# A float32 gather, a token-major router and a 24th weight tile in a two-block model with 32 experts

## The chip, the cores and the metric

One core of one Trainium2 chip. The metric is the device time of one execution in microseconds; the figure for a kernel is the median of its runs.

## The reference

Two blocks on x of 256 tokens by 1024: a hybrid layer (four mixers, then a gated FFN), and a block of pooling with differential attention, cross attention and a mixture of experts. The change lies in the last part:

```python
logits = (xt @ w_router + b_router).astype(jnp.float32)   # 256 x 32
top_val, top_idx = lax.top_k(logits, TOP_K)               # TOP_K = 4
gates = jax.nn.softmax(top_val, axis=-1)
...
hb = clamped_swiglu(xb @ w_gu[e] + b_gu[e])    # xb: the tokens of expert e, w_gu[e]: 1024 x 2048
yb = hb @ w_down[e] + b_down[e]                # w_down[e]: 1024 x 1024
return yb * g[:, None].astype(yb.dtype)        # added into the tokens' rows
```

where xt is x, normalised by its root mean square and a gain. Everything is float32, so one expert has 12 MiB of weights and the 32 experts 384 MiB.

## The kernel before

All of the first block and the attention come first, to about 750 us; the rest of the run is the mixture of experts. x lies in x_t, two halves of 128 tokens by 1024.

**Router.** hT is x transposed and scaled. Eight products lps (L1301) give the logits with experts on the partitions, four partial sums side by side; ScalarE copies them (lsb, L1304), and two products lp with ident4 (L1307) add the partial sums and turn them to tokens on partitions. rm is 1/rms. VectorE makes the logits lg (L1312), the top 8 and their indices (L1358, L1361), casts the indices (L1364), compares them with iota_e into oh (L1369) and sums that to selb, the mask of chosen experts (L1372). pos (L1376 to L1378) counts, by a triangular matrix, each token's place among its expert's. seed (L1337) first adds x into the four accumulators acc.

**Gather.** Each expert has CAP = 64 places. For two experts at a time, one_hot (L1447) builds Sg, a bf16 matrix that holds a 1 where a token has a place; a chunk (L1472) is x's 128 columns times Sg. So that bf16 products are exact enough, x times 1/rms is split ahead into three bf16 parts xs: POOL multiplies and subtracts (L1346, L1348, L1350), ScalarE rounds (L1347, L1349). A chunk is six products, and ScalarE or VectorE evacuates it into xgg (L1478, L1476).

**Experts.** front(e) is gue (L1529), eight pieces of weights of 1 MiB, each with four float32 products of 512 columns; swiglu transposes (gte, L1545) and activates; dn_product (dne, L1571) takes four pieces of 1 MiB; scatter (L1581) adds the result into acc. The program writes gue of expert e+1 ahead of dne of expert e. The chunks of the next two experts stand between the pieces of dne of every even expert; those of experts 0 and 1 stand in gue of expert 0. A stop near 1530 us belongs to the overflow branch after expert 25, where SP reads the largest count.

**Weight tiles.** Each piece is loaded by SP's queue (ld in in_turn, L1493 and L1495) in the order of the program into a tile of slot_tile. The string SLOTS names the pool of each following tile, cyclically: 23 letters. A letter is a pool of one buffer, but "x" has two and "p" six. The pools x and p exist from the start of the kernel; the others lie where earlier stages' tiles lay. A load waits for the last reader of its buffer, and as SP issues in order, everything behind it waits too.

```python
SLOTS = "xxolkmnpppgfhppdeijpcba"
pool = slots[SLOTS[slot[0] % len(SLOTS)]]
return pool.tile([P, 2 * D], F32, tag="raw", name=f"raw{rawc[0]}")
```

b_down, 32 by 1024, is loaded after expert 1's weights by load_b_down into a corner of x_t (bd4), and add_b_down reads it after dne of expert 2 and after dne of expert 4. gs, u_ and gT, small results of an expert, lie in x_t as well, which nobody reads once it is split and seeded.

Of the kernel before, what the change touches and what calls it, by code (L numbers as in the profile page):

```python
# [22 lines left out]
P = 128  # L23
# [8 lines left out]
SLOTS = "xxolkmnpppgfhppdeijpcba"  # L32
# [11 lines left out]
def kernel(ctx: ExitStack, tc: tile.TileContext, A, out, probe=None, stop=None):  # L44
# [1266 lines left out]
    for b in range(2):  # L1311
        last["V"] = V.scalar_tensor_tensor(lg[:, b, :], lp2[:, b * NE:(b + 1) * NE], rm[:, b:b + 1], brt,  # L1312
                                           op0=ALU.mult, op1=ALU.add)
# [20 lines left out]
    def seed():  # L1334
        for b in range(2):
            for h in range(2):
                PE.matmul(acc[b][h], ident, x_t[:, b, half(h)], start=True, stop=False)  # L1337


    xsp = [mp.tile([P, 2, D], BF16, name=f"xs{i}") for i in range(3)]  # L1340
    xr = small.tile([P, D], F32, tag="xg", name="xr", bufs=1)
    for h in range(2):
        for b in range(2):
            hi, mid, lo = (t[:, b, half(h)] for t in xsp)
            rest = xr[:, half(b)]
            G.tensor_scalar(rest, x_t[:, b, half(h)], rm[:, b:b + 1], 0.0, op0=ALU.mult, op1=ALU.add)  # L1346
            S.copy(hi, rest)  # L1347
            G.tensor_tensor(rest, rest, hi, op=ALU.subtract)  # L1348
            S.copy(mid, rest)  # L1349
            G.tensor_tensor(lo, rest, mid, op=ALU.subtract)  # L1350
# [3 lines left out]
    i8 = small.tile([P, 2, 8], U32, tag="i8s", name="i8s", bufs=1)  # L1354
    fi = small.tile([P, 2, TOPK], F32, tag="fi", name="fi", bufs=1)
    st_ = small.tile([P, 2, 8], F32, tag="st_", name="st_", bufs=1)
    for b in range(2):
        V.max(out=t8[:, b, :], in_=lg[:, b, :])  # L1358
    V.tensor_scalar(st_[:, :, 4:5], t8[:, :, 0:1], -1.0, None, op0=ALU.mult)
    for b in range(2):  # L1360
        V.max_index(i8[:, b, :], t8[:, b, :], lg[:, b, :])  # L1361
        S.activation(st_[:, b, 0:TOPK], t8[:, b, 0:TOPK], AF.Exp, bias=st_[:, b, 4:5],
                     accum_out=st_[:, b, 5:6])
    V.tensor_copy(fi, i8[:, :, 0:TOPK])  # L1364
    oh = small.tile([P, 2, NE, TOPK], F32, tag="SG", name="oh", bufs=1)
# [9 lines left out]
    seed()  # L1375
# [6 lines left out]
    def gates():  # L1382
        V.reciprocal(st_[:, :, 6:7], st_[:, :, 5:6])
        for b in range(2):
            V.tensor_scalar(st_[:, b, 0:TOPK], st_[:, b, 0:TOPK], st_[:, b, 6:7], None, op0=ALU.mult)
            V.tensor_tensor(oh[:, b], oh[:, b], st_[:, b, 0:TOPK].unsqueeze(1).to_broadcast([P, NE, TOPK]),
                            op=ALU.mult)
        V.tensor_reduce(out=gate, in_=oh, axis=AX.X, op=ALU.add)

        V.tensor_scalar(gateh, gate, 0.5, None, op0=ALU.mult)  # L1390

        rest = oh[:, 0].rearrange("p e k -> p (e k)")[:, :2 * NE].rearrange("p (b e) -> p b e", b=2)
# [7 lines left out]
    gateh = mp.tile([P, 2, NE], F32, name="gateh")  # L1400
# [12 lines left out]
    yh, yl, sT = (small.tile([P, w], F32R, tag=t, name=t, bufs=1) for t, w in (("yh", 512), ("yl", 512), ("sT", T)))  # L1413


    xa = x_t.rearrange("p b d -> p (b d)")
    u_ = xa[:, 1024:1536].rearrange("p (h c s) -> p h c s", h=2, c=4)
    bd4 = xa[:, 1792:]

    def load_b_down():  # L1420
        for q in range(4):
            ld(bd4[q * NE:(q + 1) * NE, :], A["b_down_2"][0, :, q * 256:(q + 1) * 256])

    def add_b_down(odd):

        g4 = small.tile([P, 2, 4, NE], F32, tag="SG", name="g4", bufs=1)
# [12 lines left out]

    def one_hot(pos_cols, n, name, s_=None):  # L1440

        if s_ is None:
            s_ = small.tile([P, 2, n, 2, CAP], BF16, tag="S_", name=f"S{name}")
        io = iota_s.unsqueeze(1).unsqueeze(1).to_broadcast([P, n, 2, CAP])
        for b in range(2):
            pos = pos_cols[:, b, :].unsqueeze(2).unsqueeze(3).to_broadcast([P, n, 2, CAP])
            last["V"] = V.tensor_tensor(s_[:, b], io, pos, op=ALU.is_equal)  # L1447
        return s_
# [13 lines left out]
    def gather(s_, n, name, xg=None):  # L1462
# [4 lines left out]
        def chunk(c, on_v=False):  # L1467
            po = ps(f"xg{name}_{c}", "tr")
            i = 0
            for part in xsp:  # L1470
                for b in range(2):
                    PE.matmul(po[:, :n * CAP], part[:, b, c * P:(c + 1) * P],  # L1472
                              s_[:, b, :, 0, :], start=i == 0, stop=i == 5)
                    i += 1
# [58 lines left out]
    def gu_out(pgu, name, gs=None):  # L1533
        if gs is None:
            gs = xa[:, :D]
# [55 lines left out]
    def group(g):  # L1591
        st["S", g] = one_hot(pos1[:, :, g * GR:(g + 1) * GR], GR, f"g{g}")
        st["xg"], chunk = gather(st["S", g], GR, f"g{g}")
        return chunk
# [7 lines left out]
    def slots_of(e):  # L1602
        g, o = divmod(e, GR)
        st["gslot", e] = turn_slots(st["S", g][:, :, o], gate3[:, :, e, :], f"e{e}")

    chunk = group(0)
    gs = front(0, {k: [lambda k=k: chunk(k + 1)] if k else [lambda: chunk(0), lambda: chunk(1)] for k in range(7)})
# [3 lines left out]
    def overflow():  # L1611
# [3 lines left out]
        with tc.If(most > CAP):  # L1615
            with tc.For_i(0, NE, 1) as e:
                ne = nc.values_load(cnt_i[0:1, bass.ds(e, 1)], min_val=0, max_val=T)
                with tc.If(ne > CAP):
# [6 lines left out]
                    os_ = small.tile([P, 2, 1, 2, CAP], BF16, tag="S_", name="os_")  # L1625
# [65 lines left out]
    junk = xa[:, :D]  # L1691
# [43 lines left out]
```

## Time and profile before

| | |
|---|---|
| median of 3 runs | 1711.63 us (1710.82 to 1713.21) |
| profiled execution | 1708.49 us, its span 1706.8 us |
| mean granted TensorE clock | 0.994 |
| TensorE busy | 1604.7 us (94%) |
| VectorE, ScalarE, POOL busy | 734.0, 516.6, 233.4 us |
| DMA | 527.66 MB, mean 309 GB/s |

The numbers further down are of the profiled execution, in us from the start of its span. A busy TensorE is not one at its peak: a float32 product of 512 columns is two records, and its weight load, PEld, overlaps. The GB/s row tells what the 16 DMA engines moved. The waits name what ended each idle stretch of a queue. The DMA share is that of the 16 engines.

### The profile page before, as it was taken

The numbers are of one execution on the slowest core, as the hardware profiler recorded it, in microseconds if no ns is written. First come the engines' busy times: TensorE is split into PE (matmuls) and PEld (weight loads), VectorE is DVE, ScalarE is ACT, GpSimd is POOL, SyncE is SP. The second block draws the span as 40 slices with busy tenths as digits, with TensorE's granted clock in tenths as the row PEclk, the third lists the DMA queues.
The fourth block names the chain that finished last, engine by engine and source line by source line (L and its number), as shares of the span: only waits on it lengthen the run. The fifth ranks groups of instructions, "written<-read, shape, count | busy, mean of one in ns | idle before, by whom it ended". The sixth has DMA issues, their size and how long they took to land. (4 is left out here: it accounts for less than half of the span.)

```text
span 1706.8 us, 24097 instructions
## 1 busy us (share of the span) xinstructions
PE 1604.7 (94%) x9539; PEld 972.9 (57%) x9540; DVE 734.0 (43%) x1606; ACT 516.6 (30%) x973; POOL 233.4 (14%) x332
## 2 busy tenths in 40 slices
PE   8899999999999999989999999999999998889896
PEld 8887799989999888963333333333333333223332
DVE  5967654667777776551222122212221222112122
ACT  4465554555565555541110111101100110001011
POOL 6988412200011000030000000000000000000000
PEclk9999999999999999999999999999999999999999
DMA  9842355655554535678999999999999999999997
GB/s 283 266 161 69 106 185 185 221 189 187 189 192 165 186 122 183 259 301 348 416 417 418 415 418 416 417 417 416 418 415 419 416 417 418 416 364 417 415 415 289
DMA packets 182676, 527.66 MB, mean 309 GB/s; under 512 B 13649, under 2 KB 101758, under 8 KB 149758
## 3 DMA queue, kind: packets, MB, share of 16 engines
q1 hardware_dynamic: 182558, 526.06, 80.4%
q8 instruction: 77, 1.26, 0.3%
q14 instruction: 41, 0.34, 0.1%
HBM read 524.95 MB, written 4.22 MB: 310 GB/s over the span
## 5 line engine op out<-in xcount | busy, mean ns | idle before, releaser
L1529 PE MATMUL gue<-raw,xgg 128*64 128x512 f32 x2032 | 464.0, 600 | 8.7 <-DMA raw<-in_w_gu_dram 8.6
L185 DVE TENSOR_TENSOR wl<-raw,wh 128x1024 fp32r<-128x1024 f32 (+3 forms) x218 | 273.4, 1256 | 177.4 <-ACT wh L184 176.8
L184 ACT CAST wh<-raw 128x1024 fp32r<-128x1024 f32 (+2 forms) x220 | 227.8, 1036 | 255.2 <-PE g L193 64.4
L1529 PEld LDWEIGHTS gue<-raw,xgg 128*64 128x64 f32 x2032 | 135.4, 137 | 272.1 <-issue 233.9
L1571 PE MATMUL dne<-raw,x_t 128*64 128x512 f32 x1024 | 243.2, 602 | 4.6 <-DMA raw<-in_w_down_dram 2.4
L1476 DVE TENSOR_SCALAR xgg<-xgg,v_c 128x128 f32<-128x128 f32 x120 | 42.1, 351 | 308.2 <-PE gue L1529 178.6
L1537 ACT COPY x_t<-gue 128x512 f32<-128x512 f32 x62 | 36.3, 585 | 328.8 <-PE gue L1529 328.8
L1699 POOL TENSOR_TENSOR ssl<-ssl,nhalf 128x1 f32<-128x1 f32 x2 | 1.1, 562 | 933.3 <-DVE ssl L1698 933.3
L1571 PEld LDWEIGHTS dne<-raw,x_t 128*64 128x64 f32 x1024 | 64.6, 136 | 112.2 <-issue 92.1
L1551 DVE TENSOR_TENSOR x_t<-gte,bgu 128x256 f32<-128x256 f32 x62 | 26.3, 425 | 223.6 <-ACT x_t L1537 158.1
L1472 PEld LDWEIGHTS <-xs 128*128 128x128 bf16 x768 | 46.2, 97 | 104.7 <-issue 102.6
L1472 PE MATMUL xgg<-Sg,xs 128*128 128x128 bf16 x768 | 65.0, 220 | 30.9 <-DVE xgg L1476 24.9
L209 ACT ACTIVATE yh<-dne,gslote 128x512 fp32r<-128x512 f32 x32 | 22.0, 687 | 234.0 <-PE dne L1571 234.0
L379 POOL TENSOR_TENSOR convo<-convo,prod 128x256 f32<-128x256 f32 x90 | 76.9, 854 | 7.4
L192 PE MATMUL g<-h_h,wh 128*128 128x256 f32 x256 | 73.1, 286 | 0.0
L193 PE MATMUL g<-h_l,wh 128*128 128x256 f32 x256 | 73.1, 285 | 0.0
L194 PE MATMUL g<-h_h,wl 128*128 128x256 f32 x256 | 72.9, 285 | 0.0
L378 POOL TENSOR_SCALAR prod<-hconv,v_c 128x256 f32<-128x256 f32 x90 | 67.9, 754 | 8.6
L1557 ACT ACTIVATE x_t<-x_t 128x256 f32<-128x256 f32 x62 | 25.9, 417 | 141.7 <-DVE x_t L1555 141.7
L1545 PEld LDWEIGHTS gte<-ident,x_t 128*128 128x128 f32 x248 | 26.0, 140 | 56.9 <-issue 42.9
L1553 DVE TENSOR_TENSOR x_t<-gte,bgu 128x256 f32<-128x256 f32 x64 | 26.8, 419 | 69.7 <-PE dne L1571 69.7
L194 PE MATMUL ffv<-h_h,wl 128*128 128x256 f32 x176 | 49.9, 284 | 0.2 <-DVE wl L185 0.2
(808 smaller groups left out, 3046.5 us busy)
## 6 DMA issues: line engine op xcount, KB each, us to landing
raw<-in_w_gu_dram SPq DMA_DIRECT2D x254, 1024.0 KB
raw<-in_w_down_dram SPq DMA_DIRECT2D x138, 1024.0 KB
raw<-in_w_in_dram SPq DMA_DIRECT2D x32, 1024.0 KB
raw<-in_w_up_dram SPq DMA_DIRECT2D x22, 1024.0 KB
raw<-in_w_out_dram SPq DMA_DIRECT2D x8, 1024.0 KB
raw<-in_w_ckv_dram SPq DMA_DIRECT2D x8, 1024.0 KB
raw<-in_w_in_dram SPq DMA_DIRECT2D x13, 512.0 KB
raw<-in_w_br_dram SPq DMA_DIRECT2D x12, 512.0 KB
```

The source lines that it names most:

```text
L184: S.copy(hi, src)
L185: last["lo"] = (eng or V).tensor_sub(lo, src, hi.bitcast(F32))
L192: PE.matmul(o, wh[:, k, :], ah[:, k, :], start=first and k == 0, stop=False)
L193: PE.matmul(o, wh[:, k, :], al[:, k, :], start=False, stop=False)
L194: PE.matmul(o, wl[:, k, :], ah[:, k, :], start=False, stop=last and k == nk - 1)
L378: G.tensor_scalar(prod[0][:, :T], hconv[:, c, k:k + T], w, 0.0, op0=ALU.mult, op1=ALU.add)
L379: G.tensor_add(convo[:, c, :], convo[:, c, :], prod[0][:, :T])
L1472: PE.matmul(po[:, :n * CAP], part[:, b, c * P:(c + 1) * P], s_[:, b, :, 0, :], start=i == 0, stop=i == 5)
L1476: V.tensor_scalar(xg[:, c, :], po[:, :n * CAP], vec["ffn"][:, c:c + 1], None, op0=ALU.mult)
L1529: PE.matmul(pgu[n][cg * CAP:(cg + 1) * CAP, :], xg[:, k, col:col + CAP], w[:, cg * D + n * 512:cg * D + (n + 1) * 512], start=k == 0, stop ...
L1537: S.copy(gs[:, n * 512:(n + 1) * 512], pgu[n])
L1571: PE.matmul(po[cg * CAP:(cg + 1) * CAP, :], u_[:, k // 4, k % 4, :], w[:, k % 2, cg * 512:(cg + 1) * 512], start=k == 0, stop=k == 7)
```

## The change

The gather multiplies x_t itself, in float32, by norm_hot, a float32 matrix that holds 1/rms where a token has a place: two products a chunk instead of six, and no split of x. The one_hot in bf16 stays for the scatter, and is built per expert. The router's products have tokens on the partitions from the start (16 products, rlg). The chosen experts are found by replacing the four largest logits (match_replace) and comparing with the logits before. Half of seed stands ahead of pos, half behind it. The first chunks alternate between two PSUM tags and two engines. Since x_t stays in use, gs, u_, yh, yl and sT have tiles of their own, and b_down goes into a tile of slot_tile. SLOTS has a 24th letter.

```diff
-SLOTS = "xxolkmnpppgfhppdeijpcba"
+SLOTS = "xxolkmnpppgfhppdeijpcbaA"
...
-    lps = ps("lps", "y")
+    rlg = [ps(f"rlg{b}", tag) for b, tag in enumerate(("y", "sc"))]
     for k in range(8):
-        PE.matmul(lps[(k % 4) * NE:(k % 4 + 1) * NE, :T], wr[:, k, :], hT[:, k, :], start=k < 4, stop=k >= 4,
-                  tile_position=(0, (k % 4) * NE))
-    lsb = pn.tile([P, T], F32, tag="ahi", name="lsb")
-    S.copy(lsb, lps[:, :T])
...
+        for b in range(2):
+            PE.matmul(rlg[b][:, :NE], hT[:, k, b * P:(b + 1) * P], wr[:, k, :], start=k == 0, stop=k == 7)
...
+    V.tensor_scalar(st_[:, :, 0:1], t8[:, :, 0:1], -1.0, None, op0=ALU.mult)
+
+    V.memset(t8[:, :, TOPK:], 3.0e38)
+    for b in range(2):
+        V.match_replace(out=lx[:, b, :], in_to_replace=t8[:, b, :], in_values=lg[:, b, :], imm_value=-3.0e38)
     with nc.allow_low_precision(reason="0 or 1"):
-        V.tensor_reduce(out=selb, in_=oh, axis=AX.X, op=ALU.add)
+        V.tensor_tensor(selb, lx, lg, op=ALU.not_equal)
+    seed(0)
...
-    bd4 = xa[:, 1792:]
+    u_ = mp.tile([P, 2, 4, CAP], F32, name="u_")
+    bd = {}
 
     def load_b_down():
+        bd["t"] = slot_tile()
         for q in range(4):
-            ld(bd4[q * NE:(q + 1) * NE, :], A["b_down_2"][0, :, q * 256:(q + 1) * 256])
+            ld(bd["t"][q * NE:(q + 1) * NE, :256], A["b_down_2"][0, :, q * 256:(q + 1) * 256])
...
-        gT = xa[:, 1024:1280]
+        bd4, gT = bd["t"][:, :256], bd["t"][:, 256:512]
...
+    def norm_hot(pos_cols, n, name):
+
+        s_ = small.tile([P, 2, n, CAP], F32, tag="SX", name=f"SX{name}", bufs=1)
+        for b in range(2):
+            for o in range(n):
+                last["V"] = V.tensor_scalar(s_[:, b, o, :], iota_s, pos_cols[:, b, o:o + 1], rm[:, b:b + 1],
+                                            op0=ALU.is_equal, op1=ALU.mult)
         return s_
...
+            for b in range(2):
+                PE.matmul(po[:, :n * CAP], x_t[:, b, c * P:(c + 1) * P], s_[:, b].rearrange("p o s -> p (o s)"),
+                          start=b == 0, stop=b == 1)
...
+    first = {k: [lambda k=k: chunk(k + 1, k % 2 == 0, ("tr", "y")[(k + 1) % 2])] for k in range(1, 7)}
+    first[0] = [lambda: chunk(0), lambda: chunk(1, True, "y")]
+    first[1].append(lambda: seed(1))
+    gs = front(0, first)
```

SP's queue at the start of the experts, before (raw366 to raw373 are the first weights of expert 2; the names in brackets are the semaphores that the load waits for, DMAHW an earlier load's landing, PE TensorE):

```order
L1493 DMA raw366_8868<-in_w_gu_2_dram 128x2048 [waits DMAHW2_49,PE_49]
L1493 DMA raw367_8870<-in_w_gu_2_dram 128x2048 [waits DMAHW3_49,PE_49,Activation_49]
L1493 DMA raw368_8872<-in_w_gu_2_dram 128x2048 [waits DMAHW4_49,DVE_49]
L1493 DMA raw369_8874<-in_w_gu_2_dram 128x2048 [waits DMAHW5_49,PE_49]
L1493 DMA raw370_8876<-in_w_gu_2_dram 128x2048 [waits DMAHW6_49,PE_49]
```

The same place now:

```order
L1466 DMA raw366_8786<-in_w_gu_2_dram 128x2048 [waits DMAHW2_49,PE_49]
L1466 DMA raw367_8788<-in_w_gu_2_dram 128x2048 [waits DMAHW3_49]
L1466 DMA raw368_8790<-in_w_gu_2_dram 128x2048 [waits DMAHW4_49,DVE_49,PE_49]
L1466 DMA raw369_8792<-in_w_gu_2_dram 128x2048 [waits DMAHW5_49]
L1466 DMA raw370_8794<-in_w_gu_2_dram 128x2048 [waits DMAHW6_49,PE_49]
```

raw367 waits for no product any more, raw369 goes into the new letter's pool without a wait for TensorE, and raw370, where raw369 was before, waits for gue's first piece of expert 0.

SP's queue at expert 5's gue (raw403 to raw410) and expert 4's dne (raw411 to raw414) now, where b_down holds the name raw378; a load that no wait for TensorE is shown for is covered by an earlier load's:

```order
L1468 DMA raw403_9215<-in_w_gu_2_dram 128x2048 [waits DMAHW2_49,PE_49]
L1468 DMA raw404_9217<-in_w_gu_2_dram 128x2048 [waits DMAHW3_49]
L1468 DMA raw405_9219<-in_w_gu_2_dram 128x2048 [waits DMAHW4_49]
L1468 DMA raw406_9221<-in_w_gu_2_dram 128x2048 [waits DMAHW5_49]
L1468 DMA raw407_9223<-in_w_gu_2_dram 128x2048 [waits DMAHW6_49,PE_49]
L1468 DMA raw408_9225<-in_w_gu_2_dram 128x2048 [waits DMAHW7_49,PE_49]
L1468 DMA raw409_9227<-in_w_gu_2_dram 128x2048 [waits DMAHW0_49]
L1468 DMA raw410_9229<-in_w_gu_2_dram 128x2048 [waits DMAHW1_49]
L1468 DMA raw411_9299<-in_w_down_2_dram 128x2x1024 [waits DMAHW2_49]
L1468 DMA raw412_9301<-in_w_down_2_dram 128x2x1024 [waits DMAHW3_49]
L1468 DMA raw413_9303<-in_w_down_2_dram 128x2x1024 [waits DMAHW4_49,PE_49]
L1468 DMA raw414_9305<-in_w_down_2_dram 128x2x1024 [waits DMAHW5_49]
```

Before, the same down pieces are one number lower, and each load has a wait of its own, on the reader 23 tiles back:

```order
L1495 DMA raw410_9394<-in_w_down_2_dram 128x2x1024 [waits DMAHW2_49,PE_49]
L1495 DMA raw411_9396<-in_w_down_2_dram 128x2x1024 [waits DMAHW3_49,PE_49]
L1495 DMA raw412_9398<-in_w_down_2_dram 128x2x1024 [waits DMAHW4_49,PE_49]
L1495 DMA raw413_9400<-in_w_down_2_dram 128x2x1024 [waits DMAHW5_49,PE_49]
L1495 DMA raw414_9511<-in_w_gu_2_dram 128x2048 [waits DMAHW6_49,PE_49]
```

Now one of them alone, raw413, waits for TensorE, as raw403, raw407 and raw408 do. These four go into pool p.

TensorE between the router and gue of expert 0 (acc is seed, stri the triangular matrix of pos, xs_8492 the first part of x), before:

```order
L1337 MATMUL acc_8486<-x_t,ident 128x512
L1337 MATMUL acc_8487<-x_t,ident 128x512
L1337 MATMUL acc_8488<-x_t,ident 128x512
L1337 MATMUL acc_8489<-x_t,ident 128x512
L1376 LDWEIGHTS stri
L1376 MATMUL pos_ps<-selb,stri 128x32
L1377 LDWEIGHTS stri
L1377 MATMUL pos_ps<-selb,stri 128x32
L1378 LDWEIGHTS stri
L1378 MATMUL pos_ps<-selb,stri 128x32
L1472 LDWEIGHTS xs_8492
L1472 MATMUL xgg_0_8568<-Sg_8550,xs_8492 128x128
```

The same place now (SXg is norm_hot's matrix):

```order
L1323 MATMUL acc_8487<-x_t,ident 128x512
L1323 MATMUL acc_8488<-x_t,ident 128x512
L1343 LDWEIGHTS stri
L1343 MATMUL pos_ps<-selb,stri 128x32
L1344 LDWEIGHTS stri
L1344 MATMUL pos_ps<-selb,stri 128x32
L1345 LDWEIGHTS stri
L1345 MATMUL pos_ps<-selb,stri 128x32
L1323 MATMUL acc_8489<-x_t,ident 128x512
L1323 MATMUL acc_8490<-x_t,ident 128x512
L1446 MATMUL xgg_0_8539<-SXg_8519,x_t 128x128 x2
L1446 MATMUL xgg_1_8543<-SXg_8519,x_t 128x128 x2
```

pos stands behind half of seed instead of all of it, the other half stands between pos and the first chunk, and a chunk is two products on x_t.

## Rows read from the trace of the kernel before

**Rows 1.** The page, part 2: GB/s moved in 40 equal slices of 42.7 us.

```profile
GB/s 283 266 161 69 106 185 185 221 189 187 189 192 165 186 122 183 259 301 348 416 417 418 415 418 416 417 417 416 418 415 419 416 417 418 416 364 417 415 415 289
```

**Rows 2.** Windows: length, each engine's busy time (count), TensorE's clock, DMA share, GB/s.

```profile
900.00:1000.00 100.00, 94.58 (x510) 34.91 (x510) 24.05 (x68) 9.64 (x20) 0.00 (x0) 1.00 1.02 417
1400.00:1500.00 100.00, 88.19 (x462) 29.93 (x458) 20.42 (x57) 9.02 (x18) 0.00 (x0) 1.00 1.02 417
```

**Rows 3.** Waits of SP's queue in 1400 to 1500 us: total, times, longest.

```profile
SPq L1495 <- DMA raw<-in_w_down_dram: 31.9, 15, 2.2
SPq L1495 <- DMA raw<-in_w_gu_dram: 31.2, 18, 2.8
```

**Rows 4.** The chain that ended last, one step: start, length.

```profile
1662.63 19.85 DMA raw<-in_w_gu_dram
```

**Rows 5.** Windows around the router, columns as in rows 2.

```profile
754.00:764.40 10.40, 7.96 (x40) 4.45 (x39) 7.13 (x18) 4.60 (x12) 8.89 (x11) 1.00 0.83 334
764.40:778.00 13.60, 10.07 (x57) 3.89 (x58) 6.03 (x15) 2.92 (x7) 3.52 (x3) 0.75 0.33 126
766.00:770.00 4.00, 1.63 (x8) 0.82 (x9) 3.86 (x10) 0.90 (x3) 1.92 (x2) 0.50 0.00 0
786.00:802.00 16.00, 16.00 (x80) 5.50 (x78) 4.18 (x13) 2.38 (x5) 0.00 (x0) 1.00 1.00 379
```

**Rows 6.** Waits of SP's queue in 680 to 800 us.

```profile
SPq L1493 <- PE gue L1529: 28.9, 9, 14.3
SPq L1493 <- PE lp L1307: 5.2, 1, 5.2
```

**Rows 7.** Timeline of SP's queue, issues of loads: start, length.

```profile
757.33 0.81 SPq L1493 DMA_DIRECT2D raw<-in_w_gu_dram  x2
...
772.47 0.33 SPq L1493 DMA_DIRECT2D raw<-in_w_gu_dram  x1
...
897.66 0.38 SPq L1495 DMA_DIRECT2D raw<-in_w_down_dram  x1
```

**Rows 8.** Timeline, router to expert 0: start, length, engine, [idle before <- releaser].

```profile
753.65 0.88 DVE L1291 TENSOR_SCALAR hT<-mt_t,v_c 128x256 f32<-128x256 f32 x2 [0.20 <-ACT hT L1289]
...
756.71 0.53 PE L1307 MATMUL lp<-ident,lsb 128*128 128x32 f32 x4
...
757.08 0.91 PE L117 MATMUL warm<-nhalf 128*128 128x128 f32 x6
...
757.35 0.41 DVE L1312 SCALAR_TENSOR_TENSOR lg__8424<-lp,rm,brt 128x32 f32<-128x32 f32 x2 [2.81 <-PE lp L1307]
...
757.83 3.68 PE L1337 MATMUL acc<-x_t,ident 128*128 128x512 f32 x8
...
757.97 0.18 DVE L1361 FIND_INDEX8 i8s<-t8s,lg__8424 128x8 uint32<-128x32 f32 x1
...
759.35 2.36 DVE L1369 TENSOR_TENSOR oh<-iota_e,fi 128x128 f32<-128x128 f32 x2
...
761.75 0.42 DVE L1372 TENSOR_REDUCE selb<-oh 128x64 bf16<-128x256 f32 x1
...
765.48 2.44 POOL L1350 TENSOR_TENSOR xs<-xr,xs 128x512 bf16<-128x512 f32 x2
...
769.04 0.20 DVE L1390 TENSOR_SCALAR gateh<-gate 128x64 f32<-128x64 f32 x1
...
769.10 3.33 PE L1529 MATMUL gue<-first,xgg 128*64 128x512 f32 x8
```

**Rows 9.** Timeline of TensorE: gather chunk, gue of expert 3, dne of expert 2.

```profile
847.50 0.51 PE L1472 MATMUL xgg<-Sg,xs 128*128 128x128 bf16 x6
...
847.94 10.52 PE L1529 MATMUL gue<-raw,xgg 128*64 128x512 f32 x48
...
865.83 1.94 PE L1571 MATMUL dne<-raw,x_t 128*64 128x512 f32 x8
```

**Rows 10.** Window before the router, columns as in rows 2.

```profile
702.00:706.00 4.00, 4.00 (x28) 3.50 (x27) 2.82 (x8) 2.46 (x7) 0.00 (x0) 1.00 1.02 428
```

More of the change, by code (lines that the diff above doesn't have):

```diff
@@ L1311 @@
     for b in range(2):
-        last["V"] = V.scalar_tensor_tensor(lg[:, b, :], lp2[:, b * NE:(b + 1) * NE], rm[:, b:b + 1], brt,
+        last["V"] = V.scalar_tensor_tensor(lg[:, b, :], rlg[b][:, :NE], rm[:, b:b + 1], brt,
                                            op0=ALU.mult, op1=ALU.add)
@@ L1332, with seed @@
     G.tensor_copy(ident_b, ident)
[L1334 to L1350, printed above, removed]
-    t8 = small.tile([P, 2, 8], F32, tag="t8s", name="t8s", bufs=1)
[L1354 to L1365, printed above, removed]
+    def seed(b):
+        for h in range(2):
+            PE.matmul(acc[b][h], ident, x_t[:, b, half(h)], start=True, stop=False)
+    t8 = small.tile([P, 2, 8], F32, tag="t8s", name="t8s", bufs=1)
+    lx = small.tile([P, D], F32, tag="gs", name="lx", bufs=1)[:, :2 * NE].rearrange("p (b e) -> p b e", b=2)
+    st_ = small.tile([P, 2, 4], F32, tag="st_", name="st_", bufs=1)
     selb = mp.tile([P, 2, NE], BF16, name="selb")
@@ L1382, in gates @@
     def gates():
-        V.reciprocal(st_[:, :, 6:7], st_[:, :, 5:6])
         for b in range(2):
[L1385 to L1388, printed above, removed]
+            S.activation(lx[:, b, :], lg[:, b, :], AF.Exp, bias=st_[:, b, 0:1])
+            V.scalar_tensor_tensor(gate[:, b, :], lx[:, b, :], 1.0, selb[:, b, :], op0=ALU.mult, op1=ALU.mult,
+                                   accum_out=st_[:, b, 1:2])
+        V.reciprocal(st_[:, :, 2:3], st_[:, :, 1:2])
+        for b in range(2):
+            V.tensor_scalar(gate[:, b, :], gate[:, b, :], st_[:, b, 2:3], None, op0=ALU.mult)
+        gateh = small.tile([P, 2, GR, CAP], F32, tag="SX", name="gateh", bufs=1).rearrange(
+            "p b o s -> p (b o s)")[:, :2 * NE].rearrange("p (b e) -> p b e", b=2)
         V.tensor_scalar(gateh, gate, 0.5, None, op0=ALU.mult)
-        rest = oh[:, 0].rearrange("p e k -> p (e k)")[:, :2 * NE].rearrange("p (b e) -> p b e", b=2)
+        rest = lx
         with nc.allow_low_precision(reason="three parts carry the 24 bits"):
@@ L1438, in add_b_down, with one_hot @@
                           start=False, stop=False, tile_position=(q * NE, 0))
-    def one_hot(pos_cols, n, name, s_=None):
-        if s_ is None:
-            s_ = small.tile([P, 2, n, 2, CAP], BF16, tag="S_", name=f"S{name}")
+    def one_hot(pos_cols, n, name):
+        s_ = small.tile([P, 2, n, 2, CAP], BF16, tag="S_", name=f"S{name}", bufs=1)
         io = iota_s.unsqueeze(1).unsqueeze(1).to_broadcast([P, n, 2, CAP])
@@ L1446, in one_hot @@
             pos = pos_cols[:, b, :].unsqueeze(2).unsqueeze(3).to_broadcast([P, n, 2, CAP])
-            last["V"] = V.tensor_tensor(s_[:, b], io, pos, op=ALU.is_equal)
+            V.tensor_tensor(s_[:, b], io, pos, op=ALU.is_equal)
+        return s_
+    def norm_hot(pos_cols, n, name):
[4 more added lines that the diff above has]
+                                            op0=ALU.is_equal, op1=ALU.mult)
         return s_
@@ L1465, in gather, with chunk @@
             xg = small.tile([P, 8, n * CAP], F32, tag="xg", name=f"xg{name}", bufs=1)
[L1467 to L1474, printed above, removed]
+        def chunk(c, on_v=False, tag="tr"):
+            po = ps(f"xg{name}_{c}", tag)
+            for b in range(2):
+                PE.matmul(po[:, :n * CAP], x_t[:, b, c * P:(c + 1) * P], s_[:, b].rearrange("p o s -> p (o s)"),
+                          start=b == 0, stop=b == 1)
             if on_v:
@@ L1534, in gu_out @@
         if gs is None:
-            gs = xa[:, :D]
+            gs = small.tile([P, D], F32, tag="gs", name=f"gs{name}", bufs=1)
         for n in range(2):
@@ L1591, in group @@
     def group(g):
-        st["S", g] = one_hot(pos1[:, :, g * GR:(g + 1) * GR], GR, f"g{g}")
-        st["xg"], chunk = gather(st["S", g], GR, f"g{g}")
+        pos_cols = pos1[:, :, g * GR:(g + 1) * GR]
+        st["xg"], chunk = gather(norm_hot(pos_cols, GR, f"g{g}"), GR, f"g{g}")
         return chunk
@@ L1602, in slots_of @@
     def slots_of(e):
-        g, o = divmod(e, GR)
-        st["gslot", e] = turn_slots(st["S", g][:, :, o], gate3[:, :, e, :], f"e{e}")
+        st["gslot", e] = turn_slots(one_hot(pos1[:, :, e:e + 1], 1, f"e{e}")[:, :, 0], gate3[:, :, e, :], f"e{e}")
     chunk = group(0)
-    gs = front(0, {k: [lambda k=k: chunk(k + 1)] if k else [lambda: chunk(0), lambda: chunk(1)] for k in range(7)})
+    first = {k: [lambda k=k: chunk(k + 1, k % 2 == 0, ("tr", "y")[(k + 1) % 2])] for k in range(1, 7)}
+    first[0] = [lambda: chunk(0), lambda: chunk(1, True, "y")]
+    first[1].append(lambda: seed(1))
+    gs = front(0, first)
     with behind({"V": last["V"]}):
@@ L1631, in overflow @@
                         V.tensor_scalar(pc, pc, float(CAP), None, op0=ALU.subtract)
-                        s_ = one_hot(pc, 1, f"o{blk}", os_)
-                        _, chunk = gather(s_, 1, f"o{blk}", oxg)
+                        _, chunk = gather(norm_hot(pc, 1, f"o{blk}"), 1, f"o{blk}", oxg)
+                        s_ = one_hot(pc, 1, f"o{blk}")
                         gslot = turn_slots(s_[:, :, 0], gc, f"o{blk}")
@@ L1690 @@
     ssl = mp.tile([P, 3, 2], F32, name="ssl")
-    junk = xa[:, :D]
+    junk = x_t[:, 0, :]
     outs = (work[:, :D], x_t[:, 1, :])
```

21 lines of the change are left out of this document (3 added, 18 removed).

## The prediction

> **What bounds the kernel now.** I began with the page: its GB/s row stands at 415 to 419 from the slice at about 810 us to the last but one, except for one of 364 [rows 1]. TensorE is nearly full too, and the windows say which of the two sets the end. From 900 to 1000 and from 1400 to 1500 us the transfers run at 417 GB/s, while TensorE's busy time falls from 94.6 to 88.2 of 100 us [rows 2]: late in the run it waits. For whom, the waits say: in 1400 to 1500 us SP's loads wait 63 us for earlier loads to land [rows 3]. The chain that ended last passes through a load of 19.9 us shortly before the last expert's products [rows 4]. The weight stream sets the end, and **every gap in it after about 750 us is permanent**, since nothing runs faster than 417 afterwards to make it up. One MiB is 1.0486 MB, so 2.515 us. TensorE is the quicker side until it has eaten the buffers: SP's ring of tiles is full in the early experts, and there a load waits for the product that frees its tile.
>
> The question is therefore where the stream stops now, and where it will stop. Now it stops at the router: 334 GB/s in 754 to 764.4 us, 126 in 764.4 to 778 with nothing at all in 766 to 770, and 379 in 786 to 802 [rows 5]. Against 417 that loses 10.4 x (1 - 334/417) = 2.1, 13.6 x (1 - 126/417) = 9.5 and 16 x (1 - 379/417) = 1.5 us, 13.0 in all. The cause is SP's waits: 14.3 us for the first product gue (expert 0) and 5.2 for the second router product lp [rows 6]. The load that takes the tile of gue's first piece was issued at 772.47, a run of two at 757.33 [rows 7]. When it came, 22 tiles were loaded, all others landed (764.4), and the queue was empty.
>
> **The router, part by part.** gue starts at 769.10 because its x arrives through a chain [rows 8]: the copy of lps and lp (to 757.24), logits, top 8, indices, a cast, two compares of 2.36 us, a sum ending at 762.17, pos, Sg, and then the third bf16 part of x, which POOL ends at 767.92. The first product of expert 0 then runs for 3.33 us instead of 1.94 [rows 9], with the clock at 0.50 in 766 to 770, where TensorE is busy 1.63 of 4 us [rows 5].
>
> - Removed: the POOL and ScalarE split of x (the 767.92), ident4, the lsb copy and lp, cast, compares and sum.
> - Added: 16 products 128x32 for the token-major logits. Each is two records, by lp's four in 0.53 us 0.13 each [rows 8]. A quarter fits between the transposes; 24 records, 3.1 us, follow from about 753.4 on (VectorE's hT at 753.65 comes behind ScalarE's first): the last ends at 756.5, well behind the last hT (754.5). Then logits and top 8 (0.6, from 757.35 to the first index search at 757.97), a negation and memset of 0.2 at most each, two match_replace (no row; the nearest in kind is the index search, 0.18 each; bounds 0.3 to 1.0 for both, I take 0.5) and a compare of 0.25: selb at 758.3, against 762.17.
> - TensorE's own queue is then the later one: seven warm products (14 records of 0.13, 1.8 us) and the first half of the seed, which stands ahead of pos: 3.68/2 = 1.8 us, to 760.1. Then pos (0.3), its evacuation (0.2, as the row of 128x64, and as much before it starts), norm_hot as four operations of 0.20 (the same row), all beside the second half of the seed, 1.8: the first gather starts at about 762. The seeds keep TensorE busy, so I take the full clock.
> - Two chunks (0.5 each; the first one's evacuation runs beside the second), and 1.94 for the first piece: **gue's first piece done at 765, not 772.47**, bounds 762.5 to 768.
> - The 24th tile lets one more load (2.5 us) go before that wait, and the wait on lp is gone: the queue runs dry at 764.4 - 2.1 + 2.5 = 764.8, so just when the next load is issued. From issue to data it was 1.5 us: what 126 GB/s moved in 13.6 us takes 4.1 at 417, so the stream ran again from 778 - 4.1 = 773.9. The stream goes on at 766.3 instead of 773.9, with one load more behind it: a gain of 7.6 + 2.5, **10 us here**.
>
> **What takes it back: the b_down tile.** In before, b_down goes into a corner of x_t. Now load_b_down takes a tile of the ring. By the string of letters it is raw378, the 33rd tile, letter p, a pool of six buffers shared by six of each 24 tiles. It is read at expert 2 and again at expert 4, so it is held for two experts while the ring turns; the p pool has five buffers left, and each p load takes the buffer of a later predecessor. The order of SP shows it: around it loads carry no wait for TensorE and p loads do, because those waits cover all others. raw403 takes the buffer of raw383 (20 back), raw408 of raw389 (19 back), and raw413, the third down piece of expert 4, that of raw401, the third down piece of expert 3, **only 12 loads back**. SP is one queue in order, so raw414 and all behind it stand behind that wait.
>
> When is raw401's product done? In before the load that waits for dne's third piece of expert 3 was issued at 897.66, and the one for gue's first at 772.47 [rows 7]: 125.2 us of TensorE's own pace, since the ring is full there. In after the same stretch holds 22 gather chunks of two f32 products instead of six bf16 ones. Six bf16 take 0.50 us [rows 9]; two f32 ones are four records, 0.15 each at most by the run of six in 0.91 [rows 8], so 0.4 to 0.6; I add 0.05 each, 1.1 us. So raw413 is issued at 765 + 125.2 + 1.1 = 891.3, and its data start at 892.8.
>
> Those rows show an f32 product at 128 columns as two records. The Trainium skill (FP8 and Floating Point Precision, TensorE Precision Notes) says true FP32 takes four passes through the array, so eight against six here, which speaks against the change; by it the chunk would grow by a third, an estimate of 0.17 us on the 0.50, 3.7 us over 22 chunks, and the raw413 time 2.6 us later than I have it.
>
> When is the stream out of work? 42 pieces lie between the restart and raw413, so 766.3 + 42 x 2.515 + 0.6 (b_down's small rows, an estimate, part of the 1.5 above) = 872.5. On the way raw403 waits for gue of expert 3 (fifth piece at about 853 in before, rows 9, so 846.5 now, data at 848, against a stream at 847.4: 0.6 lost) and raw408 for dne of expert 2 (third piece 867.7, so 861 and data at 862.5, against 860.5: 2.0 lost): dry at 875.1. **The gap is 892.8 - 875.1 = 17.7 us.**
>
> **The sum.** In before the same piece started at 764.4 + 9.5 + 43 x 2.515 + 1.5 = 883.5. In after at 892.8: **9.3 us later**. Behind it the stream runs at 417 as before, the stop at the overflow branch (the slice of 364, rows 1) and the tail stay. When raw401 is done TensorE still has eleven loaded tiles (raw402 to raw412). Between the two issues of 125.2 us it finishes 54 pieces, 2.3 us each, so that is 25 us of work, and raw413 lands 4 us later: it doesn't starve. It loses its lead sooner, which costs nothing. The one-hot built per expert is on VectorE, busy 24 of 100 us [rows 2]; were that cover gone, its two compares an expert would stand before ste. gates() loses work, and gs, u_, yh, yl and sT only change their place: nothing. The profiled execution was 1708.49 us, so it would become 1717.8; the median of the runs is 3.1 above it, and with it 1711.63 + 9.3 = **1720.9**.
>
> Bounds: first piece 762.5 to 768; chunks -0.07 to +0.2 each, -1.5 to +4.4; issue to data 1.5 to 2.5. raw413's data 887.7 to 900, 4.2 to 16.5 us later: 1716 to 1728.
>
> **Rivals.**
> - *The stream makes the gap up* (faster). If 417 is not the stream's own limit, loads after the gap may run quicker, and only the router's gain is left. For it: 428 GB/s in 702 to 706 us [rows 10]. To recover 20 us over the 800 us that follow needs 417 x 820/800 = 427; above 422 the change is no loss. Then 13.0 less 2.1 stays: about 1701. Against: in 1400 to 1500 us SP waits for landings alone and has all the loads it may issue, and the rate is 417 all the same. 0.08. The Trainium skill (DMA: Bandwidth & Descriptors, Where 436 GB/s comes from) names 435 GB/s as the ceiling and about 358 for transfers from HBM; the 417 measured here is above the second, and by the first an estimate of 2.41 us for 1 MiB would bring this rival about.
> - *Gain and gap cancel.* If the first piece comes at 762 and expert 3 costs TensorE less than 0.3 us per chunk, or the wait on raw401 is shorter by some overlap, the piece is less than 3.4 us late: 1711 to 1715. 0.08.
> - *The gap goes on.* raw432 takes raw413's tile, raw437 waits for b_down's last use; if TensorE falls behind after the gap and drops its clock as at 766 (0.50), another 5 to 8 us are lost: 1726 to 1731. Against: these uses lie some 20 us ahead of the loads. 0.12.
> - *The change doesn't act*: were raw413 free earlier, the order of SP would show no wait there; it does. No chance of its own.
>
> **How the numbers follow.** Forecast (later by 9.3) 0.72. A measurement tells some 0.2%, 3.4 us, from no change. The range reaches from the middle of the cancelling case to the middle of the last: 1713 to 1729. Slower 0.72 + 0.12 = 0.84, same 0.08, faster 0.08.
>
> **What would show it.** Right: gue starts at 762 to 764; no idle stream beyond 2 us near 765; one stretch of about 18 us without transfers from about 875 to 893, SP waiting there for dne; 417 behind it, last weights landed some 9 us later than now. Wrong: no gap at 875, rates above 420 behind it, or TensorE waiting for weights right after 893.

## The result, and the profile after

| | before | changed |
|---|---|---|
| median of 5 runs each | 1710.85 us (1709.91 to 1713.21) | 1720.13 us (1719.18 to 1722.0) |
| ratio, 95% interval | | 1.0059, [1.0048, 1.0070] |
| span of the profiled execution | 1706.8 us | 1720.3 us |
| TensorE busy | 1604.7 us | 1630.8 us |

The changed kernel is 9.3 us slower, where 9.3 was forecast (1720.9 us, from the three-run median of 1711.63). The page of the changed kernel shows where: its GB/s row, against [rows 1].

```profile
GB/s 287 254 163 62 111 184 184 219 190 182 195 182 174 192 108 195 267 346 396 413 214 419 416 418 417 416 417 416 418 417 417 417 416 418 415 375 418 415 416 289
```

The router's gain shows in the slices from 731 to 817 us, 346 and 396 where [rows 1] have 301 and 348. The slice from 860 to 903 us has fallen to 214, where [rows 1] have 417. The later ones are as before, but for 375 instead of 364 at the overflow branch. Finer windows (columns as in [rows 2]; this execution came to the router 2.85 us later than that of before, as the sum into x_t further down shows):

```profile
754.00:764.40 10.40, 10.40 (x71) 8.08 (x70) 5.36 (x28) 2.71 (x8) 0.98 (x2) 1.00 1.02 417
766.00:768.00 2.00, 2.00 (x14) 0.78 (x12) 0.00 (x0) 0.00 (x0) 0.00 (x0) 1.00 0.71 291
768.00:770.00 2.00, 2.00 (x10) 0.62 (x11) 0.00 (x0) 0.37 (x1) 0.00 (x0) 1.00 0.89 242
844.00:874.00 30.00, 27.70 (x138) 11.26 (x134) 6.33 (x20) 2.17 (x4) 0.00 (x0) 1.00 0.92 370
874.00:900.00 26.00, 24.86 (x123) 8.65 (x119) 7.42 (x23) 3.59 (x8) 0.00 (x0) 1.00 0.32 129
890.00:895.00 5.00, 4.38 (x24) 1.58 (x24) 1.86 (x5) 0.61 (x2) 0.00 (x0) 1.00 0.00 0
900.00:1000.00 100.00, 94.56 (x460) 36.25 (x461) 25.31 (x80) 9.57 (x19) 0.00 (x0) 1.00 1.02 418
```

754 to 764.4 us is now at 417, where [rows 5] had 334, and of the empty stretch at 766 to 770 a dent is left: 0.6 us lost in 766 to 768 and 0.8 in 768 to 770. Then come the losses that weren't there. 844 to 874 at 370 loses 30 x (1 - 370/417) = 3.4 us, 874 to 900 at 129 loses 18.0, and from 890 to 895 nothing at all moves. SP's queue in 800 to 900 us (waits), and its issues:

```profile
SPq L1468 <- PE dne L1544: 57.4, 10, 27.8
...
767.36 2.84 SPq L1466 DMA_DIRECT2D raw<-in_w_gu_dram  x2
...
896.88 0.88 SPq L1468 DMA_DIRECT2D raw<-in_w_down_dram  x2
```

One wait for dne lasts 27.8 us, from 869 to 896.88: the load of raw413. The timeline of the router in the changed kernel, from the last sum into x_t on:

```profile
753.84 1.37 DVE L756 TENSOR_TENSOR x_t<-dt,x_t 128x512 f32<-128x512 f32 x2 [1.08 <-PE dt L201]
...
760.09 0.17 DVE L1337 MATCH_REPLACE8 lx<-t8s,lg__8422 128x32 f32<-128x32 f32 x1
...
760.25 0.18 DVE L1337 MATCH_REPLACE8 lx<-t8s,lg__8422 128x32 f32<-128x32 f32 x1
...
760.46 0.23 DVE L1339 TENSOR_TENSOR selb<-lx,lg__8422 128x64 bf16<-128x64 f32 x1
...
760.72 1.88 PE L1323 MATMUL acc<-x_t,ident 128*128 128x512 f32 x4
...
764.32 1.05 PE L1446 MATMUL xgg<-SXg,x_t 128*128 128x128 f32 x8
...
765.38 1.94 PE L1502 MATMUL gue<-first,xgg 128*64 128x512 f32 x8
```

In before that sum starts at 750.99:

```profile
750.99 1.37 DVE L756 TENSOR_TENSOR x_t<-dt,x_t 128x512 f32<-128x512 f32 x2 [1.08 <-PE dt L201]
```

So this execution came to the router 2.85 us later, in code that the change doesn't touch. That is spread and not the change: the same sum starts at 750.76 in both_at_2 (below), whose code and tiles are those of the changed kernel up to there. Less that, selb is ready at 757.8 (762.17 in [rows 8]) and gue starts at 762.5 instead of 769.10, at full clock: its first piece takes 1.94 and not 3.33 us. Behind gue the price of the float32 gather shows, in dne of expert 2:

```profile
857.04 1.94 PE L1544 MATMUL dne<-raw,u__8518 128*64 128x512 f32 x8
858.91 0.71 PE L1446 MATMUL xgg<-SXg,x_t 128*128 128x128 f32 x4
860.07 0.71 PE L1446 MATMUL xgg<-SXg,x_t 128*128 128x128 f32 x4 [0.44 <-DVE xgg L1449]
860.71 1.94 PE L1544 MATMUL dne<-raw,u__8518 128*64 128x512 f32 x8
```

The same place in before:

```profile
859.34 1.94 PE L1571 MATMUL dne<-raw,x_t 128*64 128x512 f32 x8
861.21 0.51 PE L1472 MATMUL xgg<-Sg,xs 128*128 128x128 bf16 x6
862.16 0.50 PE L1472 MATMUL xgg<-Sg,xs 128*128 128x128 bf16 x6 [0.44 <-DVE xgg L1476]
862.59 1.94 PE L1571 MATMUL dne<-raw,x_t 128*64 128x512 f32 x8
```

A chunk takes 0.71 us, where six bf16 products took 0.51; from one piece of dne to the next it is 3.67 us, where before has 3.25. Every second chunk waits 0.44 us for VectorE's evacuation of the one ahead, in both kernels. The end is as it was, in the chain that ended last: loads, then the last expert.

```profile
1657.53 18.52 DMA raw<-in_w_down_dram
1676.45 19.61 DMA raw<-in_w_gu_dram
1696.10 1.94 PE gue L1502 x8
```

### The profile page after: what moved, and what is told of

The parts are those of the page before. It is cut to its first block, busy times and chain, and to the rows that moved or that the text cites. A ratio compares the mean times of both kernels' runs of the same rounds, so it can differ in the third digit from the quotient of the medians.

```text
span 1720.3 us, 23615 instructions
## 1 busy us (share of the span) xinstructions
PE 1630.8 (95%) x9295; PEld 1000.6 (58%) x9296; DVE 742.5 (43%) x1702; ACT 510.2 (30%) x958; POOL 220.4 (13%) x319
## 5 line engine op out<-in xcount | busy, mean ns | idle before, releaser
L1544 PE MATMUL dne<-raw,u__8518 128*64 128x512 f32 x1024 | 242.2, 602 | 2.1 <-SPq L1590 1.2
L1510 ACT COPY gse<-gue 128x512 f32<-128x512 f32 x62 | 36.3, 586 | 326.4 <-PE gue L1502 326.4
L1544 PEld LDWEIGHTS dne<-raw,u__8518 128*64 128x64 f32 x1024 | 65.2, 136 | 108.9 <-issue 95.7
L1446 PEld LDWEIGHTS xgg<-SXg,x_t 128*128 128x128 f32 x512 | 66.8, 190 | 103.5 <-issue 51.6
L1446 PE MATMUL xgg<-SXg,x_t 128*128 128x128 f32 x512 | 91.0, 300 | 25.8 <-DVE xgg L1449 25.0
L1524 DVE TENSOR_TENSOR gse<-gte,bgu 128x256 f32<-128x256 f32 x62 | 26.3, 425 | 193.6 <-ACT gse L1510 139.3
L1530 ACT ACTIVATE gse<-gse 128x256 f32<-128x256 f32 x62 | 25.8, 417 | 139.7 <-DVE gse L1528 136.4
L1518 PEld LDWEIGHTS gte<-ident,gse 128*128 128x128 f32 x248 | 26.0, 140 | 56.9 <-issue 42.9
L1526 DVE TENSOR_TENSOR u__8518<-gte,bgu 128x256 f32<-128x256 f32 x64 | 26.8, 419 | 67.7 <-PE dne L1544 67.7
```

The costliest lines, as they stand in the source:

```text
L1446: PE.matmul(po[:, :n * CAP], x_t[:, b, c * P:(c + 1) * P], s_[:, b].rearrange("p o s -> p (o s)"), start=b == 0, stop=b == 1)
L1510: S.copy(gs[:, n * 512:(n + 1) * 512], pgu[n])
L1544: PE.matmul(po[cg * CAP:(cg + 1) * CAP, :], u_[:, k // 4, k % 4, :], w[:, k % 2, cg * 512:(cg + 1) * 512], start=k == 0, stop=k == 7)
```

## The experiments

My theory (A): b_down's tile, held in the ring for two experts, makes SP wait for a product of only 12 loads ago, and this stop costs more than the router gains. The first rival (B): the 26 us that TensorE's busy time grew by, the float32 gather, set the end. The first four runs tell these apart; their answer made a second theory (A2: the stop costs what A says, but once it is gone TensorE's work sets the end), which seven more tested, and the last run takes out the 24th tile. Each run has a ratio to the kernel before, measured beside it; before's median there was 1710.2 to 1711.0 us every time, so the times of different runs can be set side by side to within about 1 us.

**both_at_1, both_at_2: the tile given back earlier.** From the changed kernel:

```diff
-        if e in (2, 4):
-            add_b_down(e // 2 - 1)
+        if e == 1:            # both_at_2: e == 2
+            add_b_down(0)
+            add_b_down(1)
```

> The changed kernel with both halves of b_down added after dne of expert 1. Now the tile is free as early as a weight tile in its place would be: each load takes the buffer of the one 24 back. Theory A: no wait of SP for TensorE costs stream time behind 770 us, neither the 18 us nor the 3.4 us: about 1699, 12 us faster than before; the windows from 844 to 900 run at 417. Theory B: 1719 to 1722 as the changed kernel.

> The changed kernel with both halves of b_down added after dne of expert 2, so that its tile is free one and a half experts earlier; its order shows raw413 waiting for that addition instead of dne of expert 3. Theory A (the held tile stops SP): the stop of 18 us near 880 goes, the two small ones at raw403 and raw408 (3.4 us lost in 844 to 874) stay: about 1702, 8 to 9 us faster than before. Theory B (the float32 gather, which raised TensorE's busy time from 1605 to 1631 us, sets the later end): no change against the changed kernel, 1719 to 1722. Theory C (the gap is made up by a stream with headroom, something else is late): 1715 or more.

Measured: 1713.56 us (ratio 1.0015, [1.0006, 1.0024]) and 1713.16 (1.0017, [1.0008, 1.0026]). Both theories miss: the time falls by 7, not by 20. Windows of both_at_1:

```profile
844.00:874.00 30.00, 27.34 (x135) 11.11 (x133) 5.99 (x22) 2.44 (x5) 0.00 (x0) 1.00 1.02 416
874.00:900.00 26.00, 24.86 (x122) 8.54 (x120) 8.05 (x25) 3.75 (x8) 0.00 (x0) 1.00 1.02 419
```

The stream does what A said, 416 and 419 where the changed kernel had 370 and 129. Yet the kernel is not 20 us shorter, and still 2.6 us behind the kernel before. The page's last slice moves only 159 GB/s instead of 289, so the weights are in early; the chain that ended last has no load in it any more:

```profile
1621.66 0.71 PE xgg L1446 x4
...
1642.41 10.45 PE gue L1502 x48
...
1666.29 7.04 PE dne L1544 x32
...
1677.59 12.17 PE gue L1502 x56
...
1694.22 7.02 PE dne L1544 x30
```

From 1621 us on the chain is TensorE without a gap: gather, dne, gue. Its own waits in the table of lines name 19.7 us for the evacuation of chunks (790 to 1490 us):

```profile
L1446 PE MATMUL xgg<-SXg,x_t 128*128 128x128 f32 x388 | 69.0, 300 | 19.7 <-DVE xgg L1449 19.7
```

both_at_2 still loses 30 x (1 - 364/417) = 3.8 us in 844 to 874, the stops at raw403 and raw408, and is no slower for it:

```profile
844.00:874.00 30.00, 27.69 (x138) 11.44 (x135) 7.49 (x23) 2.27 (x4) 0.00 (x0) 1.00 0.90 364
```

The reading is A2: with the big stop gone TensorE is the bound, and small stops in the stream are hidden. half_free and tags_free test it below.

**before_held: the held tile alone.** From the kernel before:

```diff
     def load_b_down():
+        bd["t"] = slot_tile()
...
-            ld(bd4[q * NE:(q + 1) * NE, :],
+            ld(bd["t"][q * NE:(q + 1) * NE, :256],
...
-        gT = xa[:, 1024:1280]
+        bd4, gT = bd["t"][:, :256], bd["t"][:, 256:512]
```

> The kernel before with one part of the change alone: b_down goes into a tile of the ring (23 letters), with the bf16 gather, the old router and all else as before. Its order shows raw411, the first down piece of expert 4, on the buffer of raw399, the first down piece of expert 3, 12 back. Theory A: that product ends at 892.8 in the trace of before, data 1.5 later, while the stream is there at 878.5: a stop of 15 to 16 us and 1726, slower than the changed kernel by about 6. Theory B: TensorE's work is that of before, 1711.

Measured 1727.05 us (1.0093, [1.0078, 1.0109]), 16.1 above before. The wait, and the window it makes:

```profile
SPq L1496 <- PE dne L1572: 38.7, 4, 25.7
...
874.00:900.00 26.00, 24.86 (x126) 9.25 (x126) 8.81 (x26) 3.48 (x7) 0.00 (x0) 1.00 0.44 171
```

26 x (1 - 171/417) = 15.3 us lost, with the bf16 gather and the old router. Theory A has the held tile's price right, and B is out as the cause of the stop.

**half_free, half_held: less work for TensorE.** half_free starts from both_at_1, half_held from the changed kernel.

```diff
-            for b in range(2):
-                PE.matmul(po[:, :n * CAP], x_t[:, b, c * P:(c + 1) * P], s_[:, b].rearrange("p o s -> p (o s)"),
-                          start=b == 0, stop=b == 1)
+            PE.matmul(po[:, :n * CAP], x_t[:, 0, c * P:(c + 1) * P], s_[:, 0].rearrange("p o s -> p (o s)"),
+                      start=True, stop=True)
```

> As the run with both halves of b_down after expert 1, and each gather chunk leaves out the second 128 tokens: one float32 product instead of two. Its trace showed the stream at 417 without a stop from 800 us on, and a chain that ends in TensorE alone. Theory A2 (with the tile free, TensorE is the bound, by the float32 gather's 26 us of extra work; the stream could be done near 1699): with some 0.35 us less for each of 124 chunks TensorE is 40 us quicker, the chain goes through loads again, 1698 to 1702. Theory D (the time behind the gap is lost in something else, the tail or the overflow branch): 1710 to 1714, as the run it stems from.

> The changed kernel as it is, b_down's tile held, with the same omission in the gather. Theory A2: the stop at raw413 ends when dne of expert 3 has its third piece, 22 chunks of about 0.35 us earlier, so the stop is 10 us instead of 18, and nothing else is gained since the stream sets the end there: 1711 to 1713, 10 or more slower than the same omission with the tile free. If TensorE's work set the end in the changed kernel too, it would fall to 1702 or less.

Measured 1700.12 us (0.9939, [0.9925, 0.9953]) and 1717.50 (1.0039, [1.0025, 1.0053]). The same omission is worth 13.4 us with the tile free and 2.6 with it held. The first is A2's number, and loads are back in its chain:

```profile
1634.49 18.48 DMA raw<-in_w_down_dram
1653.03 19.84 DMA raw<-in_w_gu_dram
```

The second was put at 1711 to 1713 and missed: I took 0.35 us off each chunk. The load that waits for raw401 was issued 125.4 us after the one for gue's first piece (764.18 to 889.53), against 129.5 in the changed kernel (767.36 to 896.88), so 4.2 over 22 chunks, 0.19 each; the evacuation's wait of 0.44 us stays.

```profile
764.18 4.90 SPq L1465 DMA_DIRECT2D raw<-in_w_gu_dram  x3
...
889.53 0.88 SPq L1467 DMA_DIRECT2D raw<-in_w_down_dram  x2
```

**seed_later.** both_at_1 with both halves of seed in gue of expert 0:

```diff
-    seed(0)
...
-    first[1].append(lambda: seed(1))
+    first[1].append(lambda: seed(0))
+    first[2].append(lambda: seed(1))
```

> As the run with both halves after expert 1, and both halves of seed moved behind pos, into gue of expert 0, so that TensorE is free for the first gather some 2 to 3.5 us earlier. Theory A: the load that waits for gue's first piece is issued at about 764 instead of 767.4, before the queue runs dry, so what is left of the stop at the router (2 us in 766 to 772) goes: about 1697, 2 us faster than with both after expert 1. If the clock falls in the idle stretch between pos and the gather, or the stream does not care, the same 1699 or 1 to 2 us more. Theory B: 1719 to 1722.

Measured 1712.51 us (1.0012, [1.0003, 1.0021]), as both_at_1. TensorE, the bound of this kernel, is busy for 8.00 of the 8 us from 752 on in both_at_1, and moving seed takes no work from it, so no gain is to be expected here; the run says nothing on the stream. Where the stream is the bound it was tried again, below.

**four_experts, four_seed: half as many chunks.** From both_at_1 and seed_later:

```diff
-SLOTS = "xxolkmnpppgfhppdeijpcbaA"
+SLOTS = "xxolkmnpppgfhppdeijpcba"
...
-    GR = 2
+    GR = 4
...
-        chunk = group(e // GR + 1) if e % GR == 0 else None
+        chunk = group(e // GR + 1) if e % GR == GR - 2 else None
```

> Nothing left out. Both halves of b_down after expert 1, and the gather takes four experts at a time: a chunk is still two float32 products, now of 256 columns, for twice as many experts, so half as many chunks and weight loads. Twice as large xg and norm_hot tiles leave room for 23 weight tiles only. Four records of 0.21 and the change of kinds make a chunk about 1.2 us against 2 x 0.92: 62 chunks less 0.6 each, 38 us less for TensorE. Theory A2: the stream is the bound again; one load less before the router's wait costs 2.5 us and the first chunks 1 us: 1701 to 1704, 7 to 10 faster than before. Theory D: 1711 to 1716.

> As the run with four experts at a time, and both halves of seed behind pos. Here the stream should be the bound, so the earlier first product counts, as it could not where TensorE set the end: theory A2 1699 to 1702, 2 us faster than with seed where the change has it. If seed's place doesn't count at all, the same as that run.

Measured 1709.33 us (0.9994, [0.9984, 1.0003]) and 1709.54 (0.9992, [0.9983, 1.0002]), both outside what was expected. Loads are the bound again in four_experts, its stream at 416 to 418 from 800 to 1500 us; what went wrong lies ahead of the router. Among its waits of SP in 640 to 770 us the ones for cy, a product of the cross attention, and for dt are longer than in both_at_1 (1.2 and 6.2):

```profile
SPq L1466 <- PE cy L1244: 16.6, 1, 16.6
SPq L1466 <- PE dt L201: 10.7, 1, 10.7
```

The wait for co_l is shorter in turn (18.4 for 31.2), so 27 us more, as the expectation of tags_free says, is too much; but the GB/s row has 250 in the slice from 726 to 769 us and both_at_1 340, which at 417 is 9.2 us. Larger xg and norm_hot tiles and 23 letters give the one-letter pools other places in SBUF. That these lie over tiles that the cross attention reads later is read from the waits; no run shows where a tile lies. With the stream as the bound, the 9 us are not made up.

**tags_free, tags_seed, tags_held: the evacuation's wait.** From both_at_1, seed_later and the changed kernel, in dn_product:

```diff
-                chunk(k, True)
+                chunk(k, True, ("tr", "mm")[k % 2])
```

> Nothing left out. As the run with both halves of b_down after expert 1, and the chunks in dne alternate between two PSUM tags, so that a chunk needn't wait for VectorE's evacuation of the one ahead (25 us of TensorE's idle time in that run, 0.45 for every second chunk). The tiles in SBUF lie where that run has them, unlike in the runs with four experts at a time, whose early loads waited 27 us more (cy, dt) at 700 to 754 us. Theory A2 (TensorE was the bound there by some 12 us): with 25 us less the chain goes through loads again: 1699 to 1703. If the evacuation were hidden anyway, or the change of kinds for each chunk eats it: 1709 to 1714.

> The same, and both halves of seed behind pos. Where the stream is the bound, the earlier first product is worth what is left of the stop at the router, 1 to 2 us: 1697 to 1702. If the load behind that wait isn't late any more, as much as without.

> The changed kernel with b_down's tile held as it is, and the two PSUM tags alone. Theory A2: the stream sets the end there, so TensorE's 25 us are worth only what they move raw413: 8 waits of 0.45 in groups 1 and 2, 3 to 4 us: 1716 to 1718, against 10 or more with the tile free.

Measured 1700.25 us (0.9940, [0.9926, 0.9953]), 1699.89 (0.9943, [0.9929, 0.9957]) and 1718.46 (1.0047, [1.0034, 1.0061]). tags_free beats both kernels, the one before by 10 us and the changed one by 20. Chunks run three or four in a row now, 0.53 to 0.56 us each by the records shown (TensorE's timeline, dne of expert 2), without the wait:

```profile
857.80 1.68 PE L1446 MATMUL xgg<-SXg,x_t 128*128 128x128 f32 x12
859.41 1.94 PE L1544 MATMUL dne<-raw,u__8518 128*64 128x512 f32 x8
861.27 1.87 PE L1446 MATMUL xgg<-SXg,x_t 128*128 128x128 f32 x14
```

and the chain runs through loads:

```profile
1635.97 18.93 DMA raw<-in_w_down_dram
...
1654.96 19.84 DMA raw<-in_w_gu_dram
```

With the tile held the same edit gives 1.7 us, a bit less than the least expected. Where TensorE is the bound it is worth 13.3 us (1713.56 to 1700.25; 10.2 us less busy time and 19.7 us less waiting, until loads end last), and little where the stream is. tags_seed is the same as tags_free within their spread. Counted from the start of the last sum into x_t, the load that waits for gue's first piece was issued 0.9 us earlier (764.92 - 752.33 = 12.6 against 765.02 - 751.50 = 13.5), so the move can be worth no more than that.

**letters_23: the 24th tile.** tags_free with the letter A taken out of SLOTS.

> As the run with two PSUM tags and the tile free (1700.25), with the letter A taken away again: 23 weight tiles. If the 24th tile is worth what the prediction gave it, one load before the wait on gue's first piece, and the rest of the layout doesn't matter: 2.5 us more, 1702 to 1704, lost in 764 to 776 us. Without a 24th pool all one-letter tiles move by 8 KB and lie over other tiles of the stages ahead, as they did with four experts at a time; if that decides, the loss is in 690 to 754 us, where loads wait for other products (cy, dt), and the time is 1704 to 1712. If neither matters, 1700.

Measured 1723.60 us (1.0079, [1.0066, 1.0093]): 23.3 slower than tags_free, far more than any case expected. Waits of SP in 640 to 800 us, its issues, and the window of 720 to 740:

```profile
SPq L1466 <- PE cy L1244: 41.3, 1, 41.3
...
692.82 0.42 SPq L1466 DMA_DIRECT2D raw<-in_w_gu_dram  x1
...
741.82 14.01 SPq L1466 DMA_DIRECT2D raw<-in_w_gu_dram  x12
...
720.00:740.00 20.00, 19.95 (x102) 16.47 (x101) 9.43 (x17) 9.40 (x18) 0.00 (x0) 1.00 0.00 0
```

SP stands 41.3 us on one wait for cy, a product of the cross attention, and the stream is empty for all of 720 to 740 us. From 640 to 754 us tags_free moves 28.0 MB and this kernel 18.2, and 9.8 MB at 417 GB/s are 23.5 us: all of the difference. So hardly any of it is the one tile less at 764 us; the wait ends at 741.8, 22 us ahead of that. The edit takes no work from an engine and adds none. Nor is it the order of the letters, for the load that stops is in the ring's first turn, where both kernels take the same pools in the same order. What is left is that 8 KB are gone from among the pools: the reading is that the tiles lie elsewhere, as above, and it is argued and not shown.

## Why the prediction was right

The time and its reason held. That the medians differ by the 9.3 us of the forecast to the tenth is luck: by the traces the piece behind the gap came 12.3 us later and not 9.3, and the terms traded errors. Issue and data times of the changed kernel are less 2.85 us here; windows are named as the trace has them.

- *The stream sets the end.* Right for before and for the changed kernel: half_held takes work from TensorE and tags_held its waits, and they gain 2.6 and 1.7 us. But the prediction said too much in "every gap in it after about 750 us is permanent". With the gather in float32 TensorE's own path is only some 7 us shorter than the changed kernel (both_at_1: 1713.56 us, with no load in its chain), and a gap in a stream that is ahead of it costs nothing (both_at_2).
- *The router.* First product of gue done by 764.5 (765 forecast, from 772.47). The chain behind it as told: selb 757.8 for 758.3; two replacements 0.17 and 0.18 us and their value loads 0.09 and 0.08, the 0.5 that was taken. The dent lost 1.5 us as forecast.
- *The small stops.* 3.4 us lost in 844 to 874 for 2.6.
- *raw413.* Issued at 894.0 for 891.3. This is the term that was mis-sized: TensorE's stretch grew from 125.2 to 129.5 us, 0.20 for each of 22 chunks, where "I add 0.05 each" stood. It lies at the upper bound that was kept, +0.2.
- *The gap.* 18.0 us for 17.7: it ended later than forecast, and began later as well, since b_down's rows cost the stream 2.2 us in 786 to 798 (368, 290 and 365 GB/s) instead of 0.6.
- *The piece behind it.* Its data came at 895.8 (898.6 in the trace, by the 289 GB/s in 898 to 900), 12.3 us later than the 883.5 that the prediction worked out for before, for 9.3. A count of what was moved agrees: in the 150 us from the last sum into x_t on, the transfers ran at 381 GB/s in before and 348 in the changed kernel, which is 150 x 33/417 = 11.9 us. The profiled spans differ by 13.5, 10.7 without the 2.85; about 1 us comes back at the overflow branch (379 GB/s for 371 in 1500 to 1550). Where the rest of 0.6 is stays open. Of the medians' 9.3 against 10.7 the rest is the spread of runs, some 3 us in each kernel.

The term that was too small for the gather is the one beside which the Trainium skill (FP8 and Floating Point Precision, TensorE Precision Notes) stood, four passes for a true float32 product: by it the chunk was to grow by an estimate of 0.17 us. The trace has 0.20 for a chunk between pieces of dne, nearer to the rule than to the 0.05 taken from the warm products. That the passes are the reason isn't shown: in tags_free three such chunks in a row take 0.56 us each, only 0.05 more than six bf16 products.

Of the rivals, *the stream makes the gap up* is out: behind the gap the windows stand at 416 to 418 GB/s, as in [rows 2], and not above. The 1701 given to it was out of reach as well: in both_at_1, without the gap, TensorE sets 1713.56. *The gap goes on* is out too: behind the gap TensorE was as busy as before (94.56 us of 900 to 1000, for 94.58 in [rows 2]), its clock at 1.00. That without the gap TensorE would be the next bound was not among the rivals; it doesn't touch the forecast, but it decides what one would do next.

## What to carry to other kernels

A ring of buffers is as deep as its oldest held buffer lets it be. Whatever is parked in it for longer than one turn shortens the distance of some later load, and in a queue that issues in order that one load stops all behind it; look in the order of the queue for the load whose predecessor stands closest. When a stop like this is taken away, work out the next bound ahead: here some 20 us less in the stream gave 7, and 13 more once TensorE no longer waited for evacuations. And where loads run ahead into memory that earlier stages still use, a new buffer or a larger tile can change which loads wait there (letters_23, four_experts), so read a change from the first load on whose wait is another.

## What the runs showed that was not expected

- One 8 KB pool more or less, with no operation added or removed, moved the first loads by up to 41.3 us of waiting and the kernel by 23.3 us (letters_23).
- Two float32 products of 128 columns with their weight loads take 0.71 us when they stand between pieces of dne, and 0.56 in a row of three (12 records in 1.68 us).
- A stream of 1 MiB loads on one queue holds 416 to 418 GB/s in every window read between 900 and 1500 us, in all kernels here, whether SP waits for TensorE or for landings.
